# Last gated layer of a two-layer encoder: the first sum of squares behind the second gate, an fp32 sum for the second group, the logarithm ahead of VectorE's reading, the last outputs in four stores

## The chip, the cores and the metric

The kernel runs on one core of a Trainium2 chip. A core has TensorE (matrix products, PE in the profile, with its weight loads as PEld), VectorE (DVE), ScalarE (ACT), GpSimd (POOL) and SyncE (SP, which here issues the DMAs). They run their own instruction streams in order and wait for each other through semaphores. Matrix products are accumulated in PSUM, eight banks of 128 partitions x 512 fp32; everything else lies in SBUF. The metric is the device time of one execution in microseconds, the median of several runs.

## The reference

Two layers are applied with the same weights to two groups of tokens, 512 and 256 of them, with a width of 1024. Layer 0 mixes the tokens by windowed attention, layer 1 by a gated convolution of width 3. After the mixer each layer has an MLP (1024 to 4096 and back, squared ReLU) and a gated embedding. The change lies at the end of layer 1 and in the norm that all parts share:

```python
def rms_norm(x, g):
    y = x * lax.rsqrt(jnp.mean(x * x, axis=-1, keepdims=True) + EPS)
    return y * g

def trunk(x, p, ...):
    for i in range(2):
        h = rms_norm(x, norm_mix[i])
        x = x + (window_attention(h, ...) if i == 0 else short_conv(h, ...))
        h = rms_norm(x, norm_mlp[i])
        x = x + jnp.square(jax.nn.relu(h @ mlp_w_up[i])) @ mlp_w_down[i]
        gate = jax.nn.sigmoid(rms_norm(x, norm_ple[i]) @ ple_w_gate[i])
        x = x + (p[i] @ ple_w_proj[i]) * gate
    return rms_norm(x, final_norm)
```

## The kernel before

**Layout.** x is kept transposed: eight blocks of 128 channels (partitions) by 768 tokens, the first 512 columns being the first group. An fp32 value goes through TensorE as two parts of a shorter format, `hi` and `lo`: ScalarE rounds to `hi`, VectorE takes `lo` as the rest, and three products (hi hi, hi lo, lo hi) stand for one fp32 product. That is why ScalarE and VectorE have a split for every weight and every operand, and why a 1024 x 128 product is 24 matmuls. Large products in the MLPs and the convolution (line 466) use seven products of half-sized blocks in place of eight; their sums are VectorE's work (lines 345 to 361 and 409 to 415).

**The norm.** `Norm` (from line 171) holds one root-mean-square norm. The squares of the eight blocks are added into `acc`; `acc_parts` splits it (lines 83 and 84, tiles `ah` and `al`); `sum_squares` multiplies by a matrix of ones (line 235), which leaves the sum over channels in PSUM, on every partition. `rstd_steps` returns three steps. In `logs`, VectorE reads the sum from PSUM into `v`, the mean plus EPS (line 252), ScalarE reads the same sum for the logarithm `ln` (line 254), then does the exponential `y` (line 255) and its square (line 256). `newton` (line 260) and `result` (line 267) on VectorE improve the root by one Newton step. A norm over all 768 tokens has its sum in two banks, so lines 252 and 254 run twice. The framework orders any two instructions of different engines that touch the same PSUM bank, two readers too, in the order in which the program gives them (the trace has ScalarE waiting for line 252 before line 254 six times, 8.2 us in all). There are eight such norms: before the attention, the first MLP, the first gate, the convolution, the second MLP, the second gate, and the final norm of each group of tokens.

**Order of the work.** Outside a `manual_schedule` block the framework's planner picks each engine's order from priorities and its own estimate of times. Inside such a block the order of ScalarE, TensorE and VectorE is the order of the program; SyncE's queue is still planned. The first MLP, the convolution, most of the second MLP and the last layer's second group are written in such blocks.

**The first MLP.** `up_first` (called from `up_begun`) starts it: the sum of squares, two blocks of products, then `logs()`, then the sums `s1.t13` and `s1.t42` on VectorE (lines 345 to 351), their splits, and `newton()`.

**The convolution.** `plain` in `mixer_conv` puts `logs`, `newton`, `result` and two more steps on a list of work that is done between the products of the next job, by `late`.

**The last layer.** `last_ple` splits the eight gate weights once, and keeps them. For the first group it computes the gates (line 138, tile `gate`), the sigmoid (line 1377), the product with the embedding `pr` and the add to x, and sums the squares. Then, in a hand-written block, come the second group's eight gates of 256 tokens. `gate_of(m)` issues the product (24 matmuls), the load of `pr`, VectorE's product with the norm (line 1518) and the sigmoid (line 1519); `added` multiplies with `pr` and adds to x (lines 1523 and 1524); `squared` squares on ScalarE (lines 1528 and 1530) and puts the add into `acc` (line 1531) on a list; line 1558 scales x by the final gain into `y`. Between the gates stands the first group's end: its sum of squares and norm right behind gate 0, then `stored` (lines 1538 and 1539), which scales a block of the first group's result and stores it. At the end come the second group's own sum (the split `acc` in two matmuls, and the last block's square `sq` as an fp32 product, which is two instructions on TensorE), its norm, three multiplies of `y` by the norm (line 1580; 3, 3 and 2 blocks) and three stores (line 1581). A sigmoid needs another table on ScalarE than the logarithm and the exponential; a change of table is an instruction of its own (ACT_TABLE_LOAD).

## Time and profile before

| what | us |
|---|---|
| median of 3 runs (lowest, highest) | 1687.13 (1685.48, 1689.20) |
| the profiled execution, its own time | 1689.38 |
| its span, first to last instruction | 1687.5 |
| TensorE busy in the span | 1650.1 |
| VectorE busy | 1415.1 |
| ScalarE busy | 903.9 |

A page gives the busy time of each engine, the chain of work that ended last, and the costliest groups of instructions. A row of the timeline has the start and the length in microseconds, the engine, the line, the operation, `out<-in`, and the shapes; behind it in brackets stand the idle time of the engine before it and what ended that. A row of the chain has the start, the length, the engine, the tile that is written and the line. Times count from the span's start. Neighbouring equal instructions are merged into one row with their count.

### The profile page before, as it was taken

What the parts mean: (1) busy time and instruction counts of PE and PEld (TensorE: products, weight loads), DVE (VectorE), ACT (ScalarE), POOL (GpSimd) and SP (SyncE); (2) the same over time, 40 slices, a digit from 0 to 9 for tenths busy, and PEclk for the clock granted to TensorE, in tenths of its full rate; (3) what the DMA queues carried; (4) which work ended last, traced back from release to release, by engine and by line L of the source; (5) the groups of instructions that cost most, each with busy time, mean ns of one, the idle gap of its engine ahead of it and who ended that gap; (6) DMA issues with size and microseconds to landing.
All of it is one profiled execution on the core that took longest, in us unless ns stands there. A gap on an engine that the chain in (4) does not pass through costs nothing.

```text
span 1687.5 us, 24113 instructions
## 1 busy us (share of the span) xinstructions
PE 1650.1 (98%) x9410; PEld 1590.2 (94%) x9410; DVE 1415.1 (84%) x2304; ACT 903.9 (54%) x1449; POOL 18.3 (1%) x44
## 2 busy tenths in 40 slices
PE   8999999999999999999999999999999999999996
PEld 6888788989999999999999999999999999999986
DVE  6598888889999989987888877868999898998776
ACT  6377756755455455544654334545545545554544
POOL 0211000000000000000000000000000000000000
PEclk9999999999999999999999999999999999999998
DMA  8754322212221222222312222121222122122222
GB/s 261 191 153 142 95 63 82 76 63 75 66 83 64 76 71 67 74 95 72 101 60 75 76 65 77 60 74 51 75 71 80 63 76 75 63 76 88 82 75 94
DMA packets 46820, 144.60 MB, mean 86 GB/s; under 512 B 6080, under 2 KB 9152, under 8 KB 46704
## 3 DMA queue, kind: packets, MB, share of 16 engines
q1 hardware_dynamic: 45168, 139.89, 26.1%
q0 software_dynamic: 1536, 3.15, 0.8%
q8 instruction: 74, 1.21, 0.3%
q14 instruction: 42, 0.34, 0.1%
HBM read 123.10 MB, written 10.48 MB: 79 GB/s over the span
## 4 chain that ended last, share of the span: by engine, by line
PE 60%; DVE 29%; ACT 7%; issue 3%; DMA 1%; SPq 0%; DVEq 0%; ACTq 0%
PE a L466 17%; PE mm L129 9%; PE mm L138 7%; PE b L466 4%; PE gate L138 4%; PE B L466 3%; PE C L466 3%; DVE t L361 3%; DVE wlo L445 3%; DVE y L1021 3%; DVE zlo L445 2%; DVE act L394 1%; PE pt L733 1%; PE c L466 1%; ACT y L1024 1%
## 5 line engine op out<-in xcount | busy, mean ns | idle before, releaser
L434 ACT ACTIVATE whi<-sum 128x1024 fp32r<-128x1024 f32 x67 | 70.5, 1053 | 146.8 <-PE a L466 146.8
L1024 ACT ACTIVATE y<-y 128x768 f32<-128x768 f32 x64 | 53.8, 840 | 143.1 <-DVE y L1021 143.1
L466 PE MATMUL a<-xs,whi 128*128 128x384 f32 x624 | 121.9, 337 | 0.7 <-DVE low L1660 0.7
L466 PE MATMUL a<-t,zhi 128*128 128x384 f32 x536 | 109.9, 338 | 2.2 <-ACT c L1225 2.2
L466 PEld LDWEIGHTS a<-xs,whi 128*128 128x128 f32 x624 | 110.1, 188 | 1.1 <-DVE low L1660 1.1
L466 PE MATMUL a<-t,whi 128*128 128x384 f32 x536 | 108.8, 336 | 0.0
L466 PE MATMUL b<-t,zhi 128*128 128x384 f32 x536 | 108.7, 336 | 0.0
L466 PEld LDWEIGHTS a<-t,zhi 128*128 128x128 f32 x536 | 95.1, 189 | 2.7 <-ACT c L1225 2.5
L466 PE MATMUL a<-act,whi 128*128 128x384 f32 x448 | 96.6, 337 | 0.0
L445 DVE TENSOR_TENSOR wlo<-wraw,whi 128x1024 fp32r<-128x1024 f32 x72 | 87.8, 1220 | 8.7 <-ACT whi L434 8.7
L466 PEld LDWEIGHTS a<-t,whi 128*128 128x128 f32 x536 | 94.9, 188 | 0.0
L466 PEld LDWEIGHTS b<-t,zhi 128*128 128x128 f32 x536 | 94.8, 188 | 0.0
L445 DVE TENSOR_TENSOR wlo<-sum,whi 128x1024 fp32r<-128x1024 f32 x67 | 81.9, 1222 | 10.1 <-ACT whi L434 10.1
L1281 DVE TENSOR_TENSOR x<-x,a 128x384 f32<-128x384 f32 x112 | 60.8, 553 | 33.7 <-PE a L466 33.5
L434 ACT ACTIVATE zhi<-sum 128x1024 fp32r<-128x1024 f32 x67 | 71.0, 1059 | 22.8 <-DVE sum L410 22.8
L138 PE MATMUL mm<-xs_mix,whi 128*128 128x512 f32 (+1 forms) x320 | 83.1, 342 | 0.0
L445 DVE TENSOR_TENSOR zlo<-sum,zhi 128x1024 fp32r<-128x1024 f32 x67 | 81.6, 1218 | 0.0
L466 PEld LDWEIGHTS a<-act,whi 128*128 128x128 f32 x448 | 79.9, 188 | 0.0
L434 ACT ACTIVATE whi<-wraw 128x1024 fp32r<-128x1024 f32 x72 | 75.7, 1052 | 6.1 <-PE C L466 5.7
L355 ACT ACTIVATE t<-y 128x768 fp32r<-128x768 f32 x56 | 47.1, 842 | 40.3 <-DVE y L346 29.9
L466 PE MATMUL a<-xs,wlo 128*128 128x384 f32 x312 | 67.1, 336 | 0.2 <-DVE wlo L445 0.2
L466 PE MATMUL b<-t,zlo 128*128 128x384 f32 x268 | 64.1, 344 | 3.1 <-DVE zlo L445 2.0
(336 smaller groups left out, 4489.5 us busy)
## 6 DMA issues: line engine op xcount, KB each, us to landing
wraw<-in_up SPq DMA_DIRECT2D x64, 512.0 KB, 3.5
wraw<-in_down SPq DMA_DIRECT2D x64, 512.0 KB, 3.5
wraw<-in_w_in SPq DMA_DIRECT2D x24, 512.0 KB, 3.5
wraw<-in_gate SPq DMA_DIRECT2D x16, 512.0 KB, 3.5
pj<-pjs SPq DMA_DIRECT2D x16, 384.0 KB, 3.1
wraw<-in_w_q SPq DMA_DIRECT2D x8, 512.0 KB, 4.4
wraw<-in_w_out SPq DMA_DIRECT2D x8, 512.0 KB, 3.5
x_in<-in_x SPq DMA_DIRECT2D x8, 384.0 KB, 7.3
```

The lines of the kernel that those rows point to most:

```text
L129: pe.matmul(t, lhsT=w, rhs=x[:, o:e], start=first and i == 0 and j == 0, stop=last and i == n - 1 and j == 2)
L138: pe.matmul(ps[:, o:e], lhsT=w, rhs=x[:, o:e], start=i == 0 and j == 0, stop=i == n - 1 and j == 2,)
L355: act.activation(t[0][:], (self.q1, self.q2)[i][:], AF.Copy)
L361: dve.tensor_tensor(lo[:], (self.q1, self.q2)[i][:], hi[:].bitcast(F32), ALU.subtract)
L394: dve.tensor_tensor(lo[:], self.q2[:], hi[:].bitcast(F32), ALU.subtract)
L434: act.activation(hi[:], src, AF.Copy)
L445: dve.tensor_tensor(lo[:], src, hi[:].bitcast(F32), ALU.subtract)
L466: pe.matmul(ps, lhsT=a, rhs=b, start=start and i == 0, stop=i == len(terms) - 1, skip_group_check=True)
L733: pe.transpose(pt[:, h * P : (h + 1) * P], lg[h // 2][:, h % 2, b * P : (b + 1) * P], ident[:],)
L1021: dve.scalar_tensor_tensor(t[:, o:e], src, 0.0, r[:, o:e], op, ALU.mult)
L1024: act.activation(t[:], t[:], AF.Square)
L1281: dve.tensor_tensor(t[:, o : o + H], t[:, o : o + H], f, op)
```

## The change

In `logs`, for every norm, ScalarE's logarithms are put ahead of VectorE's readings of the same sums. In `last_ple`, gate 0 of the second group is finished with its square and `y`, gate 1's product and its product with the norm are issued, and between these and gate 1's sigmoid stands the whole norm of the first group, whose sum of squares is issued behind the product of gate 1. The stores of the first group move one gate later. For the second group, the squares of blocks 0 to 5 are added into `acc`; `acc`, the square of block 6 and that of block 7 go into the sum as three fp32 products, with no split. The final multiplies and stores of the second group are four: 1, 2, 3 and 2 blocks. `y` lies in the same three slots.

```diff
             def logs():
                 self.table()
                 for t, o, e in ss:
+                    act.activation(ln[:, o:e], t, AF.Ln, scale=1.0 / D, bias=eps[:])
+                for t, o, e in ss:
                     dve.tensor_scalar(v[:, o:e], t, 1.0 / D, EPS, ALU.mult, ALU.add)
-                for t, o, e in ss:
-                    act.activation(ln[:, o:e], t, AF.Ln, scale=1.0 / D, bias=eps[:])
                 act.activation(y, ln, AF.Exp, scale=-0.5)
                 act.activation(ln, y, AF.Square)
...
-        groups = ((0, 3), (3, 3), (6, 2))
+        groups = ((0, 1), (1, 2), (3, 3), (6, 2))
...
-            adds.append(lambda: dve.tensor_tensor(second.acc, second.acc, sq, ALU.add))
+            if m < KB - 2:
+                adds.append(lambda: dve.tensor_tensor(second.acc, second.acc, sq, ALU.add))
+            else:
+                held.append(sq)
...
+        def shifted(m):
+            if m < KB - 1:
+                squared(m)
+                act.activation(y[m], x(m, s0, s1), AF.Copy, scale=gain(6, m))
+
         with tc.manual_schedule(engines={ET.Activation, ET.PE, ET.DVE}):
             parts = first.acc_parts()
-            for m in range(KB):
-                t, pr = gate_of(m)
-                if m == 0:
-                    ss = first.sum_squares(psum, parts=parts)
-                while adds:
-                    adds.pop(0)()
-                if 2 <= m < 5:
-                    stored(2 if m < 4 else 1)
+            added(0, *gate_of(0))
+            shifted(0)
+            ps = product(second, 1)
+            ss = first.sum_squares(psum, parts=parts)
+            gated1 = gate_of(1, ps, sigmoid=False)
+            logs, newton, result = first.rstd_steps(psum, ss)
+            logs()
+            newton()
+            result()
+            rf = first.r
+            t, pr = gated1
+            act.activation(t[:, :s1], t[:, :s1], AF.Sigmoid)
+            for m in range(1, KB):
+                if m > 1:
+                    t, pr = gate_of(m)
+                if m < KB - 1:
+                    while adds:
+                        adds.pop(0)()
+                stored((0, 0, 0, 2, 2, 1, 1, 0)[m])
                 added(m, t, pr)
-                if m == 0:
-                    steps = first.rstd_steps(psum, ss)
-                    steps.pop(0)()
-                if m < KB - 1:
-                    squared(m)
-                    act.activation(y[m], x(m, s0, s1), AF.Copy, scale=gain(6, m))
-                for step in steps:
-                    step()
-                steps = []
-                rf = first.r
-                if m == 5:
-                    stored(1)
-                if m == KB - 2:
-                    adds.pop(0)()
-                    parts = second.acc_parts()
+                shifted(m)
             second.last = second.gated
             second.table()
-            ss = second.sum_squares(psum, also=x(m, s0, s1), parts=parts)
+            sq = second.temp("sq")
+            dve.tensor_tensor(sq, x(m, s0, s1), x(m, s0, s1), ALU.mult)
+            ss = fresh("ss")[:, :s1]
+            terms = [second.acc, *held, sq]
+            for i, z in enumerate(terms):
+                pe.matmul(ss, lhsT=ones32[:], rhs=z, start=i == 0, stop=i == len(terms) - 1)
...
-            for yb, (m, n) in zip(held, groups):
+            for m, n in groups:
+                yb = ys[m // 3][:, m % 3 : m % 3 + n, :]
                 dve.tensor_tensor(yb, yb, rf[:, None, :].broadcast_to([P, n, s1]), ALU.mult)
                 nc.sync.dma_start(out[m : m + n, :, s0:].rearrange("m p t -> p m t"), yb)
```

More of the change, by code (lines that the diff above doesn't have):

```diff
@@ L1502, in last_ple, with gate_of @@
             first.square(m, block(first, m, gps[m] if m < 2 else None))
-        groups = ((0, 3), (3, 3), (6, 2))
-        held = [slot(i, "y", F32)[:, : n * s1].rearrange("p (m n) -> p m n", m=n) for i, (_, n) in zip(ys, groups)]
-        y = {m + i: t[:, i, :] for t, (m, n) in zip(held, groups) for i in range(n)}
+        groups = ((0, 1), (1, 2), (3, 3), (6, 2))
+        ys = [slot(i, "y", F32).rearrange("p (m n) -> p m n", n=s1) for i in ys]
+        y = {m: ys[m // 3][:, m % 3, :] for m in range(KB)}
         outs = [more.tile([P, CH], F32, tag=tag, name="o", bufs=1) for tag in ("sum0", "sum1", "zhi", "zlo")]
         left = list(range(KB))
-        adds = []
-        def gate_of(m):
-            [(ps, _, _)] = product(second, m)
+        adds, held = [], []
+        def gate_of(m, gp=None, sigmoid=True):
+            [(ps, _, _)] = gp or product(second, m)
             pr = slot(prs[m % 3], "pr", F32)
@@ L1518, in gate_of @@
             dve.tensor_tensor(t[:, :s1], ps, r[:, s0:], ALU.mult)
-            second.gated = act.activation(t[:, :s1], t[:, :s1], AF.Sigmoid).ins
+            if sigmoid:
+                second.gated = act.activation(t[:, :s1], t[:, :s1], AF.Sigmoid).ins
             return t, pr
@@ L1572, in last_ple @@
             stored(1)
-            logs, newton, result = second.rstd_steps(psum, ss)
+            logs, newton, result = second.rstd_steps(psum, [(ss, 0, s1)])
             logs()
```

## The prediction

> **What bounds the kernel now.** I read the page's head, then the chain of waits over the last layer, then the timeline of that stretch engine by engine, and last the waits around every norm, since the edit in `logs` reaches all eight of them.

> ```profile
> span 1687.5 us, 24113 instructions
> PE 60%; DVE 29%; ACT 7%; issue 3%; DMA 1%; SPq 0%; DVEq 0%; ACTq 0%
> ```

> Work that ends last is TensorE's for 60% and VectorE's for 29%: the stages differ, so each edit has to be priced where it falls. The profiled execution took 1689.38 us, 1.9 more than its span and 2.25 more than the median of the runs (1687.13). I make the sum against 1689.38 and carry the difference to the median.

> The chain at the end of the program (start, length, engine, tile, line):

> ```profile
> 1651.84 18.59 PE gate L138 x144
> ...
> 1674.05 0.43 DVE gt L1518
> ...
> 1675.40 0.44 DVE x L1524
> 1675.86 0.44 DVE sq L226
> 1676.34 1.23 PE ss L235 x2
> ...
> 1677.60 0.43 DVE v L252
> ...
> 1678.12 0.48 ACT ln L254
> ...
> 1679.52 0.44 DVE v L260
> ...
> 1680.44 0.96 DVE y L1580
> ```

> Here TensorE is the bound until the gates are done, and from 1674.05 a single file of small instructions ends the program. How long a gate's product takes is in the stretches cut from the trace (stretch, length, TensorE busy and count, clock, DMA):

> ```profile
> 1660.00:1673.30 13.30, 13.27 (x112) 1.00 0.46 153
> ```

> That is 13.27 / 112 x 24 = 2.84 for a product's 24 matmuls. The chain's gate row ends at 1670.43 with the sixth of them, so the last ends about 1673.3.

> **The change, part by part.**

> *First sum of squares behind the second gate.* The timeline between the first group's last add and the second group's second gate:

> ```profile
> 1650.62 0.49 PE L235 MATMUL ss<-ah,ones 128*128 128x512 f32 x1 [2.16 <-ACT ah L83]
> 1652.10 1.28 ACT L216 ACT_TABLE_LOAD   x1
> 1652.57 0.42 DVE L1524 TENSOR_TENSOR x<-x,gt 128x256 f32<-128x256 f32 x1
> 1653.63 0.69 ACT L254 ACTIVATE ln<-ss,eps 128x512 f32<-128x512 f32 x1 [0.26 <-DVE v L252]
> 1657.67 0.42 ACT L1519 ACTIVATE gt<-gt 128x256 f32<-128x256 f32 x1
> 1658.58 0.43 DVE L1524 TENSOR_TENSOR x<-x,gt 128x256 f32<-128x256 f32 x1
> ```

> TensorE stands 2.16 us for the sum's operand, and the following gates run behind it. With product 1 in that hole and the two sum matmuls after it, TensorE has products 2 to 7 left at about 1651.85, where before it had seven: 6 x 2.84 is 17.0, so it ends near 1669.0, 4.3 earlier. But VectorE and ScalarE now go through the same norm with one more thing ahead of it. Before, the ScalarE order from the first sigmoid was load, logarithm, exponential, square, acc, y0, load, second sigmoid: 1652.10 to 1657.67, 5.57 us. After, acc and y0 come first, and they need x0, whose add starts at 1652.57; as sq follows x in the chain by 0.46, an instruction on another engine follows by about 0.5, so ScalarE starts the same list at 1653.05 instead of 1652.10. Less the 0.26 waited for v, plus some 0.1 of lost overlap, the second sigmoid starts at 1658.5 and x1's add 0.91 later (1657.67 to 1658.58), at 1659.4: 0.85 later than before. From there each gate is a ring of VectorE and ScalarE instructions; its length is read from successive x adds of before:

> ```profile
> 1661.67 0.42 DVE L1524 TENSOR_TENSOR x<-x,gt 128x256 f32<-128x256 f32 x1
> 1664.70 0.42 DVE L1524 TENSOR_TENSOR x<-x,gt 128x256 f32<-128x256 f32 x1
> 1667.06 0.42 DVE L1524 TENSOR_TENSOR x<-x,gt 128x256 f32<-128x256 f32 x1
> 1669.20 0.43 DVE L1524 TENSOR_TENSOR x<-x,gt 128x256 f32<-128x256 f32 x1
> ```

> The ring with two stores' multiplies in it takes 3.03, with one 2.36, with none 2.14. The new order has 0, 2, 2, 1, 1, 0 of them for gates 2 to 7: 2.14 + 3.03 + 3.03 + 2.36 + 2.36 + 2.14 = 15.06, so x7's add starts at 1674.5 against 1675.40. Of TensorE's 4.3, **0.9** is left; its gates wait finished in PSUM. The first norm's v, newton and result stand ahead of gate 1's multiply on VectorE and end before the second sigmoid does; gate 1's load of pr goes out earlier with its product, and the first group's stores one gate later, on a SyncE queue where nothing behind them is due sooner: nothing for these. Bounds: if the ring ran at its shortest throughout (2.14 x 6), 3.1; if stores cost one more wait of 0.3 each, nothing.

> *Second group's squares in fp32.* The split of acc (one ScalarE and one VectorE instruction) and its two matmuls go; two more fp32 terms come, each at the 1.23 of the last row for ss. They are for acc and the square of block 6, ready by about 1671.4 and 1673.3 by the ring (1.4 after x5's add at 1670.0, 1.0 after x6's at 1672.3), so at 1.23 each they are done by 1674.6, under the 1675.4 at which the last square arrives: nothing. Without that cover 1.2 per term. The removed VectorE split stood before the last gate's multiply (1674.05), but that gain is already in the ring.

> *Logarithm ahead of VectorE's reading, last norm.* ScalarE's logarithm starts 0.52 after v (1677.60 to 1678.12); reading PSUM first it follows the matmul itself. v now runs beside the exponential; the store's multiply queued behind v holds newton by about 0.1. So **0.4**, and the final multiplies start at about 1679.1, 1.3 early.

> *Outputs in four.* SyncE's issues and the DMA engines over 1679 to 1688 us (40 slices of 0.225 us):

> ```profile
> 1681.77 1.61 SPq L1581 DMA_DIRECT2D out<-y  x3
> DMA  0149950000000001499999999999981000000000
> GB/s 0 36 191 382 355 210 27 0 0 0 0 0 0 0 0 36 164 360 305 355 360 342 346 328 355 346 342 355 337 314 55 0 0 0 0 0 0 0 0 0
> ```

> From its first byte (about 1682.4) the store runs the DMA engines full, so what counts is that first byte: a first piece of 256 columns takes 0.44 (like the x add) instead of 0.96 and so starts 0.5 sooner. At 350 GB/s its 0.13 MB lasts 0.38, less than the second multiply, so about 0.2 is lost again: **0.3**. One more issue (1.61 / 3 is 0.54) lies beside moving data. Bounds: 0.5 gained to 0.3 lost, if the fourth piece's issue shows. Together the end of the program gains 0.9 + 0.4 + 0.3 = **1.6**.

> *The same edit in the other norms.* `logs` now makes VectorE's v wait until ScalarE has read the bank, with all of VectorE's queue behind it. Where that counts:

> ```profile
> 318.43 1.02 DVE L252 TENSOR_SCALAR v<-ss 128x384 f32<-128x384 f32 x2
> 319.37 0.55 DVE L345 TENSOR_TENSOR q<-q 128x384 f32<-128x384 f32 x1
> 322.67 0.96 DVE L260 SCALAR_TENSOR_TENSOR v<-ln,v 128x768 f32<-128x768 f32 x1 [0.90 <-ACT ln L256]
> 319.82 1.05 ACT L254 ACTIVATE ln<-ss,eps 128x384 f32<-128x384 f32 x2
> 354.20 2.30 PE L466 MATMUL a<-t,zhi 128*128 128x384 f32 x8 [2.16 <-ACT c L1225]
> ```

> First MLP: ScalarE copies until its logarithms at 319.82 to 320.87, so both v end near 321.4 instead of 319.45; the sums q behind them (319.37) slip by 2.0. VectorE had 0.90 idle before newton, so newton slips by about **1.0**, and from there the chain runs through VectorE and ScalarE without a gap to the pause at 354.20, in which TensorE waits for them. So +1.0; bounds 0 (the slip is absorbed by a gap that the chain hides) and 2.0 (the idle doesn't absorb).

> ```profile
> 887.00 0.34 PE L235 MATMUL ss<-al,ones 128*128 128x384 f32 x1
> 888.20 1.05 ACT L254 ACTIVATE ln<-ss,eps 128x384 f32<-128x384 f32 x2 [2.70 <-DVE v L252]
> 900.84 1.68 PE L466 MATMUL a<-xs,whi 128*128 128x384 f32 x8 [0.75 <-DVE low L1660]
> ```

> Convolution's norm: here v came late in VectorE's queue and ScalarE sat 2.70 idle for it. The first bank is summed at about 887.0, so the logarithms start 1.2 earlier, and what follows on ScalarE and VectorE with them; TensorE's wait of 0.75 at 900.84 goes: **-0.75**, bounds -1.2 and 0.

> ```profile
> 45.24 0.46 PE rt L623 x6
> 816.77 0.56 DVE L1402 TENSOR_TENSOR gt<-gate,rstd_ple 128x384 f32<-128x384 f32 x1 [2.05 <-PE gate L129]
> 1134.57 1.23 DVE L445 TENSOR_TENSOR zlo<-wraw,zhi 128x1024 fp32r<-128x1024 f32 x1 [2.55 <-ACT zhi L434]
> 1628.93 0.69 DVE L1376 TENSOR_TENSOR gt<-gate,rstd_ple 128x512 f32<-128x512 f32 x1 [0.98 <-PE gate L138]
> ```

> The other four lie under TensorE: in the attention its transposes of the norm follow its own products (45.24), and VectorE idles 2.05, 2.55 and 0.98 us behind the other three before it is wanted. I put them at nothing, with 1 us to either side, since in parts without a hand-written order the planner may place neighbours differently.

> Sum: -1.6 + 1.0 - 0.75 = **-1.35**: 1688.0 for a profiled run like this one, **1685.8** for the median.

> The longer pause at 354.20 touches the clock, TensorE's granted clock being the third figure of each row:

> ```profile
> 351.00:354.20 3.20, 0.97 (x4) 1.00 0.02 9
> 354.20:357.78 3.58, 3.58 (x13) 0.61 0.02 5
> ```

> After a pause of 2.16 the clock was 0.61, and the twelve matmuls took 3.58 instead of about 2.1: 1.5 us. This price is already paid in before; the forecast keeps it once. [...]

> **The rivals.** (1) *TensorE's 4.3 comes through*: the ring isn't the bound, as VectorE catches up on finished gates. For: in before the last gates waited for TensorE. Against: two of the six rings take 3.03, more than the 2.84 of a product, and the ring starts with five microseconds of arrears. Then -4.3 - 0.7 + 1.0 - 0.75 = -4.75: 1682.4. (2) *The slip in the first MLP is absorbed* before 354.20. For: the chain is inferred. Against: no idle of VectorE there that ScalarE's own late work doesn't explain. -2.35: 1684.8. [...] (4) *The order isn't changed*, since both readers of a bank are ordered anyway and the planner keeps v first: then only the last layer's own edits act, -0.9 - 0.3 = -1.2: 1685.9. Against: the blocks around these norms are ordered by hand.

> **How the numbers follow.** A measurement of this kernel can tell about 0.2%, 3.4 us, from no change. Chances: forecast 0.52, (1) 0.15, (2) 0.14, (3) 0.12, (4) 0.07. Faster by over 3.4 us: (1), and 0.05 from the ends of the forecast (tail 2.2, first MLP 0, convolution 1.2) and of (2): 0.20. Slower by over 3.4: only (3) with all bounds against it: 0.04. The rest, 0.76, is within. The range leaves out most of (1) and the ends of (3): 1682.8 to 1688.9.

> **What would show it.** In the changed profile: no wait of about 2.16 at the first group's ss; TensorE's last product of the second group ending over 3 us before VectorE's multiply of it begins; rings of 3.0, 2.4 and 2.1 between x adds; ln ahead of v in all norms, and the last one straight behind ss; the first y store issued 1.5 to 1.9 earlier relative to the first group's last add. At 318 VectorE's q sums 2 us later behind v, and TensorE's pause before the `c` copy reached 1 us later; at 900 no wait for `low`. Wrong, if the last gate's multiply starts right at TensorE's end, if newton at 322 doesn't move, or if the time falls outside the range.

## The result, and the profile after

The changed kernel takes 1683.38 us (median of 22 runs, 1682.04 to 1686.98), the kernel before 1686.18 in the runs beside them (22, 1684.20 to 1689.20). The ratio is 0.9985 with a 95% interval of 0.9979 to 0.9992: **2.5 us faster**, with 1.3 and 3.5 as bounds (the two medians lie 2.8 apart; the ratio is used from here on). The forecast was 1.35 faster and sits at the edge of that interval; a gain of over 3.4 us, to which it gave 0.20, was not reached. The profiled execution took 1686.10 us against 1689.38.

The page's head and the shares of the chain that ended last, by engine:

```profile
span 1684.3 us, 24118 instructions
...
PE 61%; DVE 29%; ACT 7%; issue 3%; DMA 1%; SPq 0%; DVEq 0%; ACTq 0%
```

The shares are nearly those of before: no bound has moved over the whole, so what was won lies in single places. The last layer comes first. Its timeline after (start, length, engine, line, operation, idle before):

```profile
1648.90 0.69 DVE L84 TENSOR_TENSOR al<-acc_final,ah 128x512 fp32r<-128x512 f32 x1 [0.70 <-ACT ah L83]
...
1649.40 0.39 PE L235 MATMUL ss<-ah,ones 128*128 128x512 f32 x1
...
1652.16 1.28 ACT L216 ACT_TABLE_LOAD   x1
1653.46 0.69 ACT L252 ACTIVATE ln<-ss,eps 128x512 f32<-128x512 f32 x1
...
1654.18 0.69 DVE L254 TENSOR_SCALAR v<-ss 128x512 f32<-128x512 f32 x1 [2.55 <-ACT ln L252]
...
1656.79 0.42 ACT L1564 ACTIVATE gt<-gt 128x256 f32<-128x256 f32 x1
...
1657.70 0.43 DVE L1525 TENSOR_TENSOR x<-x,gt 128x256 f32<-128x256 f32 x1
...
1659.78 0.42 DVE L1525 TENSOR_TENSOR x<-x,gt 128x256 f32<-128x256 f32 x1
...
1662.80 0.42 DVE L1525 TENSOR_TENSOR x<-x,gt 128x256 f32<-128x256 f32 x1
...
1665.89 0.43 DVE L1525 TENSOR_TENSOR x<-x,gt 128x256 f32<-128x256 f32 x1
...
1666.36 0.87 PE L138 MATMUL gate<-xs_ple,gwr 128*128 128x256 f32 x6
...
1668.32 0.42 DVE L1525 TENSOR_TENSOR x<-x,gt 128x256 f32<-128x256 f32 x1
...
1670.74 0.42 DVE L1525 TENSOR_TENSOR x<-x,gt 128x256 f32<-128x256 f32 x1
...
1672.88 0.42 DVE L1525 TENSOR_TENSOR x<-x,gt 128x256 f32<-128x256 f32 x1
```

The 2.16 us for which TensorE stood ahead of `ss` are gone, and its last gate product ends at 1667.2, 5.6 us before the add of that gate to x begins; before, the product and that add were 2.1 apart. To compare executions here, I count from the start of `al`, the split that ends the first group's sum, which before was this row:

```profile
1650.60 0.69 DVE L84 TENSOR_TENSOR al<-acc_final,ah 128x512 fp32r<-128x512 f32 x1 [0.69 <-ACT ah L83]
```

It is 1650.60 before and 1648.90 after; a time with a plus sign below counts from it. TensorE's last product ends 18.3 behind it, where it was 22.7: 4.3 earlier. The add of x1 stands 8.80 behind it (7.98 before, so 0.82 later), the add of x7 23.98 (24.80 before, so 0.82 earlier). The span ends 35.40 behind it (36.90 before): **1.50 of the gain is in the tail.**

The chain after the last gate, with engine, tile and line:

```profile
1672.88 0.44 DVE x L1525
...
1673.33 0.44 DVE sq L1577
...
1673.81 1.24 PE ss L1581 x2
...
1675.13 0.48 ACT ln L252
...
1676.64 0.43 DVE v L260
...
1677.55 0.42 DVE y L1592
```

From the square to the logarithm it is 1.80 (1675.13 - 1673.33) where it was 2.26; the first multiply of `y` is one of 0.42 where it was one of 0.96.

The three other places of the forecast, after: VectorE in the first MLP and TensorE at its pause, then ScalarE and VectorE at the convolution's norm.

```profile
319.28 1.05 ACT L252 ACTIVATE ln<-ss,eps 128x384 f32<-128x384 f32 x2
...
319.89 1.03 DVE L254 TENSOR_SCALAR v<-ss 128x384 f32<-128x384 f32 x2 [1.92 <-ACT ln L252]
320.83 0.55 DVE L345 TENSOR_TENSOR q<-q 128x384 f32<-128x384 f32 x1
...
323.08 0.95 DVE L260 SCALAR_TENSOR_TENSOR v<-ln,v 128x768 f32<-128x768 f32 x1
...
354.61 2.77 PE L466 MATMUL a<-t,zhi 128*128 128x384 f32 x8 [2.16 <-ACT c L1225]
```

```profile
886.78 1.05 ACT L252 ACTIVATE ln<-ss,eps 128x384 f32<-128x384 f32 x2 [1.53 <-PE ss L235]
...
898.82 0.55 DVE L1672 TENSOR_TENSOR low<-a,p 128x384 f32<-128x384 f32 x1
...
899.52 1.58 PE L466 MATMUL a<-xs,whi 128*128 128x384 f32 x8
```

In the first MLP ScalarE's logarithms come 0.54 earlier than before by the span's clock (319.82), yet newton comes 0.41 later (322.67): a slip of 0.95. In the convolution the logarithms follow the sum (`<-PE ss`) and not v any more, and the wait of 0.75 for `low` is gone.

TensorE's weight loads are the same in number in all these kernels up to the last layer, and but for a few dozen of some 9500 in the same order, so the same load can be found in each trace. Its start, less that of before, gives the columns below by subtraction; the tail is the span's end counted from `al`, less the 36.90 of before. "Sum" adds the columns from the first MLP on, before rounding, and "measured" is the ratio to the kernel before times 1686.1 (us).

| kernel | up to 308 | 308 to 512 (first MLP) | 512 to 861 (first gated layer) | 861 to 904 (convolution's norm) | 904 to 1055 (second MLP) | tail | sum | measured |
|---|---|---|---|---|---|---|---|---|
| the changed kernel | -0.6 | +1.1 | -0.5 | -1.4 | -0.3 | -1.5 | -2.6 | -2.5 |
| logarithm first alone | -3.0 | +1.0 | -0.6 | -1.4 | -0.3 | -1.1 | -2.4 | -2.4 |
| last layer alone | -3.4 | +0.1 | +0.1 | 0.0 | 0.0 | -1.6 | -1.4 | -1.5 |
| changed, first MLP kept | -1.2 | 0.0 | -0.6 | -1.4 | -0.3 | -1.6 | -3.9 | -3.5 |
| gate 1 ahead of the norm | -3.0 | +0.1 | -0.6 | -1.4 | -0.3 | -2.9 | -5.2 | -5.2 |

From 1055 to `al` the profiles differ by another 0.1 or less. The first column is left out of the sums: it scatters from profile to profile, also where nothing ahead of 308 differs from before (the last layer alone), and is taken up under the last heading.

### The profile page after: what moved, and what is told of

Its sections match the earlier page's. It is cut to its first block, busy times and chain, and to the rows that moved or that the text cites. A ratio compares the mean times of both kernels' runs of the same rounds, so it can differ in the third digit from the quotient of the medians.

```text
span 1684.3 us, 24118 instructions
## 1 busy us (share of the span) xinstructions
PE 1648.6 (98%) x9412; PEld 1589.0 (94%) x9412; DVE 1414.6 (84%) x2303; ACT 902.7 (54%) x1448; POOL 18.3 (1%) x44
## 4 chain that ended last, share of the span: by engine, by line
PE 61%; DVE 29%; ACT 7%; issue 3%; DMA 1%; SPq 0%; DVEq 0%; ACTq 0%
PE a L466 18%; PE mm L129 9%; PE mm L138 8%; PE b L466 4%; PE B L466 4%; PE C L466 3%; DVE t L361 3%; DVE wlo L445 3%; PE gate L138 3%; DVE y L1021 3%; DVE zlo L445 2%; DVE act L394 1%; PE d L466 1%; PE c L466 1%; PE pt L733 1%
## 5 line engine op out<-in xcount | busy, mean ns | idle before, releaser
L434 ACT ACTIVATE whi<-sum 128x1024 fp32r<-128x1024 f32 x67 | 70.5, 1052 | 146.9 <-PE a L466 146.9
L466 PE MATMUL a<-xs,whi 128*128 128x384 f32 x624 | 121.8, 337 | 0.0
L466 PE MATMUL a<-t,zhi 128*128 128x384 f32 x536 | 110.4, 340 | 2.2 <-ACT c L1225 2.2
L466 PEld LDWEIGHTS a<-xs,whi 128*128 128x128 f32 x624 | 110.1, 188 | 0.2
L466 PE MATMUL a<-t,whi 128*128 128x384 f32 x536 | 108.8, 336 | 0.0
L466 PE MATMUL b<-t,zhi 128*128 128x384 f32 x536 | 108.7, 336 | 0.0
L466 PEld LDWEIGHTS a<-t,zhi 128*128 128x128 f32 x536 | 95.7, 189 | 2.5 <-ACT c L1225 2.5
L466 PE MATMUL a<-act,whi 128*128 128x384 f32 x448 | 96.6, 337 | 0.0
L445 DVE TENSOR_TENSOR wlo<-wraw,whi 128x1024 fp32r<-128x1024 f32 x72 | 87.7, 1218 | 8.7 <-ACT whi L434 8.7
L466 PEld LDWEIGHTS a<-t,whi 128*128 128x128 f32 x536 | 94.9, 188 | 0.0
L466 PEld LDWEIGHTS b<-t,zhi 128*128 128x128 f32 x536 | 94.8, 188 | 0.0
L445 DVE TENSOR_TENSOR wlo<-sum,whi 128x1024 fp32r<-128x1024 f32 x67 | 81.9, 1222 | 9.9 <-ACT whi L434 9.9
L434 ACT ACTIVATE zhi<-sum 128x1024 fp32r<-128x1024 f32 x67 | 71.0, 1060 | 22.7 <-DVE sum L410 22.7
L138 PE MATMUL mm<-xs_mix,whi 128*128 128x512 f32 (+1 forms) x320 | 83.0, 342 | 0.0
L445 DVE TENSOR_TENSOR zlo<-sum,zhi 128x1024 fp32r<-128x1024 f32 x67 | 81.5, 1217 | 0.0
L466 PEld LDWEIGHTS a<-act,whi 128*128 128x128 f32 x448 | 79.8, 188 | 0.0
L434 ACT ACTIVATE whi<-wraw 128x1024 fp32r<-128x1024 f32 x72 | 75.7, 1051 | 6.3 <-PE C L466 6.1
L466 PE MATMUL a<-xs,wlo 128*128 128x384 f32 x312 | 67.1, 336 | 0.2 <-DVE wlo L445 0.2
L466 PE MATMUL b<-t,zlo 128*128 128x384 f32 x268 | 64.2, 344 | 3.0 <-DVE zlo L445 1.9
```

The source lines that it names most:

```text
L138: pe.matmul(ps[:, o:e], lhsT=w, rhs=x[:, o:e], start=i == 0 and j == 0, stop=i == n - 1 and j == 2,)
L434: act.activation(hi[:], src, AF.Copy)
L445: dve.tensor_tensor(lo[:], src, hi[:].bitcast(F32), ALU.subtract)
L466: pe.matmul(ps, lhsT=a, rhs=b, start=start and i == 0, stop=i == len(terms) - 1, skip_group_check=True)
```

## The experiments

The theory is that of the forecast: the ring of VectorE and ScalarE bounds the gates, so that TensorE's earlier end is worth only what the ring lets through; in the first MLP v and all behind it on VectorE are held until the logarithms are done, for 1.0; the convolution's norm gives some back. The rivals are those of the prediction.

**Logarithm first alone.** The kernel before with the first part of the diff and nothing else:

```diff
                 for t, o, e in ss:
+                    act.activation(ln[:, o:e], t, AF.Ln, scale=1.0 / D, bias=eps[:])
+                for t, o, e in ss:
                     dve.tensor_scalar(v[:, o:e], t, 1.0 / D, EPS, ALU.mult, ALU.add)
-                for t, o, e in ss:
-                    act.activation(ln[:, o:e], t, AF.Ln, scale=1.0 / D, bias=eps[:])
```

> The kernel before with only the edit in logs, in all eight norms. Theory A (place by place, from the two profiles): +1.0 in the first MLP, -1.2 in the convolution, -0.7 in the first gated layer, -0.3 in the attention, -0.5 in the two final norms: -1.7 us, and TensorE's pause before the c copy near 354 us comes 1.0 later than in the kernel before, counted from the end of the attention. Theory B (the prediction's own terms): +1.0 - 0.75 and -0.5 in the final norms: -0.25 us. Theory C (the edit does nothing that lasts, all of the gain is the last layer's): 0.

1684.06 us, ratio 0.9986 (0.9977 to 0.9995). The slip in the first MLP and the gain in the convolution are both there (second row of the table). But the whole is 2.4 us faster, at least 0.8 by the interval, and the terms of the forecast for this edit (+1.0 - 0.75 - 0.4 in the last norm) give 0.15 faster. Of the three theories only A lies in the interval, and it too was short, by 0.7: it lacked a place in the second MLP and a part of the tail. Two places outside the tail had been put at nothing in the prediction. One is the first gated layer; VectorE and, at its end, TensorE before, then VectorE after:

```profile
817.24 0.95 DVE L1408 TENSOR_TENSOR gt<-pr,gt 128x768 f32<-128x768 f32 x1
...
859.75 0.62 PE L129 MATMUL gate<-xs_ple,wlo 128*128 128x384 f32 x2 [0.31 <-DVE wlo L84]
```

```profile
815.82 0.96 DVE L1408 TENSOR_TENSOR gt<-pr,gt 128x768 f32<-128x768 f32 x1 [0.91 <-ACT gt L1405]
817.32 0.56 DVE L1402 TENSOR_TENSOR gt<-gate,rstd_ple 128x384 f32<-128x384 f32 x1 [0.54 <-PE gate L129]
```

Before, gate 0's multiply stood behind gate 1's reading of its product, which waited 2.05 for TensorE (the row at 816.77 in the prediction). With the logarithms first the planner puts the multiply ahead, into that idle time; the add to x follows 0.8 earlier (817.79 for 818.58). From there on VectorE waits for nothing but ScalarE, and ScalarE nearly only for VectorE, up to 859.75, where TensorE waited for the split `wlo` of a weight; that wait (0.31 in the products' row, 0.63 in that of the weight loads) is gone in every kernel with the logarithms first in this layer, and there in the other two beside the kernel before (last layer alone, and the product's order alone). That VectorE carried its lead from 817 to 859 is read from the order of its rows and not tried by itself. The other place is a wait of TensorE for VectorE's `ys` at 1053.95 in the second MLP: 0.25 in the products' row and 0.57 in that of the weight loads, of which 0.29 is left in the second row and nothing in the first. In the tail 0.25 is the wait of `ln` for v in the first group's norm, 0.35 the last norm (from the end of `ss` to newton 1.59 for 1.94), and 0.52 the last sum, which the edit does not touch: 0.71 for 1.23, where the granted clock was 0.50 before (from 1675.94 to the end) and such a product takes 0.70 at a clock of 1.00 in the changed kernel (1669.76):

```profile
1671.89 0.71 PE ss L235 x2
...
1672.68 0.48 ACT ln L252
```

**The last layer alone.** The changed kernel with v first in the six norms ahead of the last layer:

```diff
-                for t, o, e in ss:
-                    act.activation(ln[:, o:e], t, AF.Ln, scale=1.0 / D, bias=eps[:])
...
+                if self.name.startswith("final"):
+                    for t, o, e in ss:
+                        act.activation(ln[:, o:e], t, AF.Ln, scale=1.0 / D, bias=eps[:])
...
+                else:
+                    for t, o, e in ss:
+                        dve.tensor_scalar(v[:, o:e], t, 1.0 / D, EPS, ALU.mult, ALU.add)
...
```

> The changed kernel with VectorE's reading first again in the six norms over all tokens; the two final norms keep the logarithm first. Theory A: only the end of the program is left of the change, -1.5 us against the kernel before, and up to the last layer every TensorE instruction stands where it stood, but for the start. Theory B: -1.6. Theory C: -2.5 or more.

1684.89 us, ratio 0.9991 (0.9982 to 0.9999). By the time alone theory C is not out (the bounds are 0.2 and 3.0 faster); by the table it is the tail's -1.6 and nothing before it. The first gated layer, the convolution and the second MLP stand as before, so their gains come from `logs`, not from the last layer's edits.

**The first MLP kept.** The changed kernel, v first in the first MLP's norm alone (`if self.name != "mlp0"` in the place of the condition above).

> The changed kernel with VectorE's reading first again in the norm of the first MLP alone. Theory A and B: 1.0 us faster than the changed kernel, -3.5 us against the kernel before, newton 0.95 earlier behind its logarithms' start, the pause near 354 us 1.0 earlier. Rival (the slip is absorbed before TensorE needs it): as the changed kernel, -2.5.

1682.07 us, ratio 0.9979 (0.9970 to 0.9988). VectorE in the first MLP:

```profile
317.34 1.02 DVE L258 TENSOR_SCALAR v<-ss 128x384 f32<-128x384 f32 x2
318.27 0.55 DVE L351 TENSOR_TENSOR q<-q 128x384 f32<-128x384 f32 x1
...
321.57 0.96 DVE L266 SCALAR_TENSOR_TENSOR v<-ln,v 128x768 f32<-128x768 f32 x1 [0.90 <-ACT ln L262]
```

The sums q follow v without a wait, newton has its 0.90 of idle again, and the column of the first MLP goes from +1.1 to 0.0: the hold costs 1.0 on the path, not 2.0 and not 0. The times alone (3.5 and 2.5 less than before, with intervals that overlap) would not tell this from the rival; the column does.

**The product's order alone.** The kernel before, with gate 1's product issued ahead of the first group's sum, and nothing else of the change:

```diff
+            ps1 = None
             for m in range(KB):
-                t, pr = gate_of(m)
+                t, pr = gate_of(m, ps1 if m == 1 else None)
                 if m == 0:
+                    ps1 = product(second, 1)
                     ss = first.sum_squares(psum, parts=parts)
```

> The kernel before with one edit: gate 1's product is issued ahead of the first group's sum of squares. TensorE's wait of 2.16 goes and its last product ends about 4.3 earlier. If the ring bounds the gates, x7's add comes 0.9 to 1.5 earlier. If TensorE's products bound them, 3 to 4.3 earlier.

1687.67 us in its one run, beside 1686.61 of the kernel before. ScalarE, VectorE and TensorE:

```profile
1655.00 1.28 ACT L1519 ACT_TABLE_LOAD   x1 [1.15 <-DVE gt L1518]
...
1657.20 0.43 DVE L1524 TENSOR_TENSOR x<-x,gt 128x256 f32<-128x256 f32 x1
...
1665.55 0.86 PE L138 MATMUL gate<-xs_ple,gwr 128*128 128x256 f32 x6
...
1673.77 0.42 DVE L1524 TENSOR_TENSOR x<-x,gt 128x256 f32<-128x256 f32 x1
```

From `al` (1648.09) TensorE's last product ends at +18.3, as in the changed kernel, 4.3 earlier than before; x1's add stands at +9.11 and x7's at +25.68, which is 0.88 *later* than before. Neither expectation was met: both had x7 earlier. TensorE's pause was no bound, and taking it away alone gains nothing. The loss is on ScalarE, where the sigmoid's table was loaded 1.15 late, behind the wait for VectorE's `gt`. In the kernel before `gt` stands behind the norm's newton and result as well, but there the load did not wait for it:

```profile
1656.37 1.28 ACT L1519 ACT_TABLE_LOAD   x1
...
1657.01 0.42 DVE L1518 TENSOR_TENSOR gt<-gate,rstd_ple 128x256 f32<-128x256 f32 x1
```

Even with that 1.15 set aside little is won: from x1's add to x7's it is 16.57 here and 16.82 before, 0.25 less.

**The split kept.** The changed kernel, with block 6's square in `acc` again and `acc` split for two short-format matmuls, as before:

```diff
-            if m < KB - 2:
+            if m < KB - 1:
...
+                if m == KB - 2:
+                    adds.pop(0)()
+                    ah, al = second.acc_parts()
...
-            terms = [second.acc, *held, sq]
+            terms = [(ones, ah), (ones, al), (ones32, sq)]
```

> The changed kernel with the second group's squares of blocks 0 to 6 added into acc and split into two parts again, as before, in place of three fp32 products. By the prediction the fp32 terms are hidden and the split costs only where VectorE's ring has it: x7's add 0.3 to 1 us later (one more add and one more split ahead of the last multiply), the sum itself as long as before. Rival (the fp32 terms cost at the end): the wait from the last square to the logarithm gets shorter.

1684.86 us in one run. The last two adds to x:

```profile
1668.06 0.42 DVE L1525 TENSOR_TENSOR x<-x,gt 128x256 f32<-128x256 f32 x1
...
1671.64 0.42 DVE L1525 TENSOR_TENSOR x<-x,gt 128x256 f32<-128x256 f32 x1
```

The last ring takes 3.58, where the changed kernel has 2.14: the split is 1.44 of the path, and x7 stands at +25.42 (`al` at 1646.22), 0.62 later than the 24.80 of before. The 1.44 is more than the 0.3 to 1 expected: the split was priced too low. So the 0.82 by which x7 gained is the split's 1.44, less the 0.62 that the rest of the new order loses. The three fp32 products cost nothing: two of them are done while TensorE waits, and the square's way to the logarithm is 1.80 with and without them.

**The first group stored last.** The changed kernel with no store of the first group in the rings; all eight follow the second group's stores:

```diff
-                stored((0, 0, 0, 2, 2, 1, 1, 0)[m])
...
                 nc.sync.dma_start(out[m : m + n, :, s0:].rearrange("m p t -> p m t"), yb)
+            stored(8)
```

> The changed kernel with all eight stores of the first group behind the last stores of the second. If the ring of VectorE and ScalarE bounds the second group's gates, each of the six rings is about 2.1 long, x7's add comes 2.2 us earlier counted from x1's add, and TensorE's last product still ends over 1 us before its multiply. If TensorE's products bound them, x7's add stays where it is. In all it is slower by about 1 to 3 us, since eight multiplies of 0.67 and their stores now end the program.

1686.15 us in one run. TensorE's last product and the last add to x:

```profile
1663.35 0.86 PE L138 MATMUL gate<-xs_ple,gwr 128*128 128x256 f32 x6
...
1667.37 0.43 DVE L1525 TENSOR_TENSOR x<-x,gt 128x256 f32<-128x256 f32 x1
```

TensorE ends at +18.3 again, but x7's add stands at +21.48 (`al` at 1645.89), 2.5 earlier than in the changed kernel: every ring is 2.07 to 2.14 now. It is VectorE's work in the ring that sets the time of a gate. The stores cost more behind the end than the rings gain: the span ends at +38.51 for +35.40, 3.1 later, about the most that was expected.

**Three outputs.** The changed kernel with `groups = ((0, 3), (3, 3), (6, 2))`.

> The changed kernel with the second group's outputs in three (3, 3 and 2 blocks). By the prediction the first store's issue comes 0.5 later behind the first of the final multiplies and the program ends 0.3 later behind it. Rival (each store costs a time of its own that shows at the end): it ends earlier behind that multiply.

1682.86 us in one run, which says nothing on so small a size by itself. The first `y` multiply in the profile:

```profile
1673.92 2.43 DVE L1592 TENSOR_TENSOR y<-y,rstd_final 128x768 f32<-128x768 f32 x3
```

The span ends at 1681.0, 7.08 behind its start; with four it is 1684.3 - 1677.55 = 6.75. The fourth store is worth 0.33. The other kernels with three stores (before, logarithm first alone, the product's order alone) have 7.1 here as well, those with four and nothing behind them 6.6 to 6.8, so it is 0.3 to 0.4.

**Gate 1 ahead of the norm.** The first MLP kept, and gate 1 finished before the first group's norm begins, with one store for each of gates 2 to 7:

```diff
-            gated1 = gate_of(1, ps, sigmoid=False)
+            t, pr = gate_of(1, ps)
+            added(1, t, pr)
             logs, newton, result = first.rstd_steps(psum, ss)
...
-            t, pr = gated1
-            act.activation(t[:, :s1], t[:, :s1], AF.Sigmoid)
-            for m in range(1, KB):
-                if m > 1:
-                    t, pr = gate_of(m)
+            for m in range(2, KB):
+                t, pr = gate_of(m)
+                if m == 2:
+                    shifted(1)
...
-                stored((0, 0, 0, 2, 2, 1, 1, 0)[m])
+                stored(1)
```

> The third kernel here with two more edits in the last layer: gate 1's sigmoid, multiply and add stand ahead of the first group's norm, where VectorE idled 2.55 us, and the first group's stores go one to each of gates 2 to 7. If the ring of VectorE and ScalarE bounds the second group's gates: one ring less behind the norm (-1.0 to -1.8) and six rings of 2.4 in place of 15.2 in all (-0.6): 1.6 to 2.4 faster than the third kernel, -5 to -6 against the kernel before. If TensorE's products bound the gates: no faster than the third kernel.

1680.91 us, ratio 0.9969 (0.9957 to 0.9980), the fastest of all: 5.2 us less than before, 2.7 less than the change by the two ratios. Against the first MLP kept it is 1.7 by the ratios and 1.3 by the tail, where 1.6 to 2.4 was expected; its two edits were not run apart. The adds of x1 and x7, and v between them:

```profile
1649.46 0.42 DVE L1531 TENSOR_TENSOR x<-x,gt 128x256 f32<-128x256 f32 x1
1651.00 0.69 DVE L255 TENSOR_SCALAR v<-ss 128x512 f32<-128x512 f32 x1 [1.12 <-ACT ln L253]
...
1668.05 0.42 DVE L1531 TENSOR_TENSOR x<-x,gt 128x256 f32<-128x256 f32 x1
```

Gate 1's sigmoid (1648.57) follows gate 0's (1646.47) with no table load between them, and both go before the two loads of 1.28 around the norm (1648.99 and 1652.32). The order saves no load: the tail has three here (the last at 1667.58) and three in the changed kernel (1652.16, 1655.49 and 1672.40). But it took gate 1 out from behind two of them. Counted from `al` (1645.41), x1's add stands at +4.05 for +8.80, and of the 4.75 a part is paid back at gate 2, which now stands behind the norm; x7's is at +22.64 for +23.98. VectorE's idle time ahead of v is 1.12 for 2.55.

## Why the prediction was right, and where its sizes were off

- *TensorE's pause at the first sum goes, and the ring takes over* (x7 0.9 earlier): measured 0.82, with x1's add 0.82 later (0.85 said) and six rings of 2.08, 3.02, 3.09, 2.43, 2.42 and 2.14, in sum 15.18 (15.06 said). Rival 1, TensorE's 4.3 comes through, fell twice: the product's order alone made x7 later, and with the stores out of the rings x7 moved while TensorE's end did not. What the forecast had wrong is what the 0.9 consists of. It called it what is left of TensorE's 4.3, and noted the removed split only as already in the ring. By the split kept, the whole of it is the split: 1.44 in the last ring, less 0.62. Yet the two belong together. In the kernel before, TensorE's last product ended at 1673.27, only 0.78 ahead of its multiply (1674.05), so without TensorE's earlier end the split's removal could have brought some 0.8 at most (an estimate from these rows). That is as much as both brought together. The removal alone was not run, so what the new order is worth beside it stays open.
- *The logarithm first in the last norm*, 0.4: from the last square to newton 3.31 (1676.64 - 1673.33) for 3.66 (1679.52 - 1675.86), so 0.35. *The fp32 terms at nothing*: shown by the split kept. The 1.23 at which the forecast priced a term came from a row at a granted clock of 0.50 (1676.34); in the changed kernel the two hidden terms take 0.70 each, at 1.00 (1669.76) and 0.96 (1671.73). *Four outputs*, 0.3: 0.33. The tail in sum: 1.50 for 1.6.
- *The first MLP, +1.0*: +1.1 in the column, q later by 2.0 against the span's shift there (1.46 by the clock of the span, on a profile that stood 0.55 earlier at 317), newton by 0.95. Rival 2 (absorbed) is out. Rival 3, to which the chances give 0.12, took a hold that stays 2.0 and 1.5 more for a second stretch at half clock. No run shows such a second stretch: newton slips by 0.95, TensorE's pause is 2.16 as before, and what follows it is one stretch of 3.41 (354.82 to 358.24; before 354.98 to 358.39), in these rows by the granted clock, 0.53 here and 0.55 before:

```profile
351.40:354.61 3.21, 0.97 (x4) 1.00 0.02 8
354.61:358.20 3.59, 3.59 (x12) 0.53 0.02 5
```

- *The convolution's norm, -0.75*: -1.4 in the column, a mis-sized term. By the loads' starts it falls in three steps, 0.2 at 876, 0.2 at 891 and 1.0 at 901. The last is the wait for `low`, which the products' row gave as 0.75 and the weight loads' row as 1.06; the one at 891 belongs to the `c` copy behind the logarithms, whose wait I had not priced. Together they are 1.2, the bound that I had named and not taken. The 0.2 at 876 stands ahead of this norm's sum (886.1), so it is not this norm's.
- *The other four norms at nothing, with 1 us either way*: -0.5 and the 0.2 just named in the first gated layer and behind it, -0.3 in the second MLP, -1.0 in sum. I had argued that VectorE idles there before it is wanted, so that a hold costs nothing. It cost nothing, but in the first gated layer the planner chose another order as well and used that idle time. That it might had been said; its sign could not be read from the trace. What shortens the wait in the second MLP was not followed further.
- *Rival 4, the order isn't changed*, is out by the rows: `ln` ahead of v at 319.28, 886.78 and 1653.46.

So -1.6 + 1.0 - 0.75 + 0 = -1.35 became -1.5 + 1.1 - 1.2 - 1.0 = -2.6, and 2.5 was measured. Direction and the bound of the tail were right, and so were the places, but for the two put at nothing; two terms were too small, by 0.45 and 1.0, both the same way. In absolute time 1685.8 was forecast and 1683.38 measured, 2.4 lower; 0.95 of that is the kernel before, which stood at 1687.13 in the three runs that the forecast started from and at 1686.18 in the 22 beside the change.

## What to carry to other kernels

A pause of the engine that is busiest is worth nothing while a ring of two others ends later. Compare the two ways as wholes, not a ring with a product: here six rings take 15.2 and six products 17.0, but the ring starts later, since x1's add stands at +8.80, and so ends 5.6 behind TensorE. Then take work out of the ring, as the split's 1.44 was. When two engines read the same PSUM bank, the one whose result is on the path should read first, but place by place: here it gains 2.2 us from the first gated layer to the second MLP (0.6 of it where the planner also changed the order) and costs 1.0 in the first MLP, where the other engine's queue is fuller. Before a table is changed on ScalarE (1.28 for each load here), finish what still needs the old one: with gate 1 ahead of the norm, and its stores one a gate, the tail was 1.3 shorter.

## What the runs showed of the hardware

*The stretches at half clock start whole multiples of 3.413 us apart in the two profiles of before and after, and lie elsewhere in another run.* TensorE around 164 us, in the kernel before, the changed one, and the product's order alone (stretch, length, busy and count, clock, DMA share, GB/s):

```profile
164.00:168.00 4.00, 4.00 (x17) 0.59 1.01 332
```

```profile
164.00:168.00 4.00, 4.00 (x18) 0.61 0.97 330
```

```profile
164.00:168.00 4.00, 4.00 (x26) 1.00 0.71 242
```

```profile
351.40:354.61 3.21, 2.86 (x12) 0.76 0.02 5
354.61:358.20 3.59, 3.59 (x17) 0.74 0.23 79
```

By these two figures its stretch is 3.41 long and starts at about 353.07 (an estimate: the half clock has 1.54 of the first row and 1.87 of the second), 1.9 ahead of the one at 354.98, which is no whole multiple. What decides whether such a stretch follows a short stop, the runs do not show. One stretch more or less moves a run by up to 1.7 us (an estimate: half of 3.41). In the column "up to 308" the two kernels with this stretch stand at -0.6 and -1.2; those without it stand at -2.5 to -4.0, the four kernels with one run among them. It speaks against comparing two profiles by their spans: of the 3.2 us between before and after, 0.6 is this column.

*A sigmoid's table load stood behind the wait for `gt` in one run, and ahead of it in two others.* In the product's order alone ScalarE waits 1.15 for `gt`, and the load of 1.28 (1655.00) and the sigmoid (1656.29) both follow that wait. In the kernel before, the load for the same sigmoid runs from 1656.37, ahead of the start of `gt` at 1657.01, and in gate 1 ahead of the norm ScalarE loads at 1652.32, for gate 2, and waits 0.52 for `gt` after that. What puts the load on one side of the wait or the other, the runs do not show.
